# Three 256-column products in place of one of 512 and one of 256, in all feature-major tiles of a two-layer decoder trunk

## The chip, the cores and the metric

The kernel runs on one core of a Trainium2 chip. The metric is the device time of one execution, in microseconds (us), taken as the median of three runs; lower is better. The engines of a core are named as the profile names them: PE (TensorE, the matrix engine), with PEld for its weight loads; DVE (VectorE); ACT (ScalarE); POOL (GpSimd); SP, which here only issues transfers. SBUF is the on-chip memory with 128 partitions, and PSUM is the small memory that PE adds its products into.

## What is computed

The reference is a trunk of two residual layers on 256 tokens of width 2048, all in float32. Each layer is a token mixer (a gMLP in the first, forgetting attention over 16 heads in the second) and then a feed-forward network with a causal convolution of width 3. Cut to the parts that the change touches:

```python
h = h + chunked_gmlp(rmsnorm(h, a_norm), w_in, v_norm, w_s, b_s, w_out)   # u * mixed(v), then w_out
...
def conv_ffn(xn, w_up, conv_w, conv_b, w_down):
    h = xn @ w_up                                   # 2048 -> 2 x 5632
    hp = jnp.pad(h, ((0, 0), (CONV_W - 1, 0), (0, 0)))
    h = sum(hp[:, k:k + S] * conv_w[k] for k in range(CONV_W)) + conv_b
    gate, val = jnp.split(h, 2, axis=-1)
    return (jax.nn.silu(gate) * val) @ w_down       # 5632 -> 2048
...
o = o * jax.nn.sigmoid(g)                           # attention: output gate, then b_w_out
return rmsnorm(h, final_norm)
```

Nearly all the arithmetic is in the matrix products of the 256 tokens with weights that are each used once.

## The kernel before

**Two parts of each number.** The products run in the type float32r, which PE streams in one pass but holds to fewer bits than float32. So every operand is split into a high part (the value rounded to float32r) and a low part (the rest), and a product of two numbers is made of three products of parts: high by high, high by low, low by high. An activation tile such as `X1` is kept as `[P, KD, 2 * T]`: for each block `kt` of 128 features, the first T = 256 columns are the high part for the 256 tokens, the next 256 are the low part. The weights are split while the kernel runs.

**The stream of chunks.** `Stream` (L40) brings in the weights as chunks of 128 x 1024 values (512 KB). In step i it issues the load of chunk i + 6 on the SP queue, splits chunk i + 3 (ACT makes `whi`, L82; DVE makes `wlo`, L83) and emits the products of chunk i, which are PE's. After each chunk's products, `advance` (L57) lets every pending generator take one step: these hold the work that follows a finished tile, and they are how that work is spread over the chunks behind it. The order of each engine's instructions is that in which this code emits them.

**Feature-major tiles.** `feat_block` (L168) computes 256 output features for all 256 tokens: two tiles (m = 0, 1) of 128 features, in the two banks of one PSUM buffer `ps` of shape `[P, 2, 512]`, of which there are three. The weights are the stationary operand, a slice of 128 x 128 from `whi` or `wlo`; the activations are the moving one. A chunk covers four blocks `kt`, so 4 x 2 slices of `whi` and as many of `wlo`. With a slice of `whi`, one product of 512 columns does both parts of the activation at once: columns 0 to 255 of the bank collect what the high activations give, columns 256 to 511 what the low ones give. With a slice of `wlo` a product of 256 columns adds to the first half. I call the first kind wide and the second narrow. The two halves of a bank are added later. In the last chunk of a block the narrow products stand ahead of the wide ones.

Seven weight arrays go through `feat_block`, in this order: `a_in_u` and `a_out` (32 chunks each), `up0` (176), `down0` (88), `b_g` and `b_out` (32 each), `up1` (176), `down1` (88): 656 chunks. One block of them is made otherwise: the last of `down1` (11 chunks) goes through `last_block` (L194), in which every product is narrow, all three kinds add into the first half of the bank, and tile m = 0 of a chunk is done before m = 1, so that the end of the kernel can begin on one tile early (`final_tile`, L317).

**Token-major tiles.** `tok_block` (L215) does `a_in_v`, `b_q`, `kvf_k` and `kvf_v`, 32 chunks each: there the activations are stationary and the weights move, 512 columns at a time. One small chunk, `kvf_f`, goes through `forget` (L547). The change leaves these alone.

**What follows a tile.** Three helpers read `ps` and add its halves:

- `scaled_sum` (L296) for `a_in_u`, `up` and `b_g` (104 blocks): ACT copies the second half of both banks to SBUF (L299, tile `half`), DVE adds the first half (L300), DVE multiplies by `rB`, the token's factor of the RMS norm (L301).
- `residual` (L303) for `a_out`, `down0` and `b_out` (24 blocks): DVE adds the two halves to the residual stream `h` in two steps (L307, L308), and then makes the next `X1`.
- `final` (L332) for blocks 0 to 6 of `down1`: the same by tile, 14 additions on L339 and 14 on L340, with squares on ACT (L341).

Of the kernel before, what the change touches and what calls it, by code (L numbers as in the profile page):

```python
# [17 lines left out]
P = 128  # L18
D = 2048
T = 256  # L20
# [112 lines left out]
def build(ctx, tc, d, out):  # L133
# [31 lines left out]
    def mm(o, a, b, start, stop):  # L165
        nc.tensor.matmul(o, a, b, start=start, stop=stop, skip_group_check=True)  # L166

    def feat_block(src, x, K, done, last=None):  # L168


        if last:
            return last_block(src, x, K, done, last)
        box = {}
        n = K // 4
        for c in range(n):
            def mult(hi, lo, c=c):
                if c == 0:
                    box["ps"] = main_ps()
                ps, xx = box["ps"], x()
                parts = (hi, lo) if c < n - 1 else (lo, hi)  # L180
                for i, part in enumerate(parts):
                    for j in range(4):
                        kt = 4 * c + j
                        for m in range(2):
                            w = part[:, j * 256 + m * P:j * 256 + (m + 1) * P]
                            if part is hi:
                                mm(ps[:, m, :], w, xx[:, kt, :], kt == 0, kt == K - 1)
                            else:
                                mm(ps[:, m, :T], w, xx[:, kt, :T], False, False)
                if c == n - 1:  # L190
                    s.start(done(ps))
            s.chunk(src[c], mult)

    def last_block(src, x, K, done, last):  # L194
        box = {}
        n = K // 4
        for c in range(n):
            def mult(hi, lo, c=c):
                if c == 0:
                    box["ps"] = main_ps()  # L200
                ps, xx = box["ps"], x()
                for m in range(2):
                    for part, half in ((lo, 0), (hi, 1), (hi, 0)):
                        for j in range(4):
                            kt = 4 * c + j
                            mm(ps[:, m, :T], part[:, j * 256 + m * P:j * 256 + (m + 1) * P],
                               xx[:, kt, half * T:(half + 1) * T], part is lo and kt == 0,
                               half == 0 and part is hi and kt == K - 1)
                    if c == n - 1:
                        last(ps, m)  # L210
                if c == n - 1:
                    s.start(done(ps))
            s.chunk(src[c], mult)
# [79 lines left out]
            for i in range(2):  # L293
                nc.vector.tensor_tensor(acc, acc, sq[:, i, :], op=OP.add)

    def scaled_sum(ps, a):  # L296

        t = small.tile([P, 2, T], F32, name="half", tag="half", bufs=2)
        nc.scalar.activation(t, ps[:, :, T:], AF.Copy)  # L299
        nc.vector.tensor_tensor(a, ps[:, :, :T], t, op=OP.add)  # L300
        nc.vector.tensor_tensor(a, a, rB[:, None, :].to_broadcast([P, 2, T]), op=OP.mult)  # L301

    def residual(p, gain):  # L303

        def done(ps):
            hh = h[:, 2 * p:2 * p + 2, :]
            nc.vector.tensor_tensor(hh, hh, ps[:, :, :T], op=OP.add)  # L307
            nc.vector.tensor_tensor(hh, hh, ps[:, :, T:], op=OP.add)  # L308
            for kt in (2 * p, 2 * p + 1):
                prep(X1, kt, gain)  # L310
            square_into_acc(p)
            yield
            if p == 7:
                yield from token_scale()
        return done
# [16 lines left out]
    def final(p, gain):  # L332

        def done(ps):
            kts = (2 * p, 2 * p + 1)
            if p < 7:
                sq = small.tile([P, 2, T], F32, name="sq", tag="sq", bufs=2)
                for m, kt in enumerate(kts):
                    nc.vector.tensor_tensor(h[:, kt, :], h[:, kt, :], ps[:, m, :T], op=OP.add)  # L339
                    nc.vector.tensor_tensor(h[:, kt, :], h[:, kt, :], ps[:, m, T:], op=OP.add)  # L340
                    nc.scalar.activation(sq[:, m, :], h[:, kt, :], AF.Square)  # L341
                if p == 0:
                    nc.vector.tensor_tensor(acc, sq[:, 0, :], sq[:, 1, :], op=OP.add)
                else:
                    for i in range(2):
                        nc.vector.tensor_tensor(acc, acc, sq[:, i, :], op=OP.add)
            for kt in kts:
                nc.scalar.activation(h[:, kt, :], h[:, kt, :], AF.Copy, scale=column(gain + kt))
            if p == 5:
                nc.scalar.activation(warm, ones, AF.Sqrt)  # L350
            if p == 7:
                for m in range(2):
                    sum_tokens(tail["sums"], tail["sq"][:, m, :], False, m == 1)
                v = small.tile([P, 2], F32, name="ts_v", tag="ts_v", bufs=2)
                nc.vector.tensor_scalar(v, tail["sums"][:, :2], 1.0 / D, EPS, op0=OP.mult, op1=OP.add)
                t = small.tile([P, 2], F32, name="rs_t", tag="rs_t2", bufs=2)
                nc.scalar.activation(t, v, AF.Sqrt)
                nc.vector.reciprocal(rcol, t)
                newton(rcol, v, t)
                mp = token_rows()  # L360
                for a, b in ((0, 2), (2, 6), (6, 11), (11, 16)):
                    nc.vector.tensor_tensor(h[:, a:b, :], h[:, a:b, :],  # L362
                                            mp[:, None, :T].to_broadcast([P, b - a, T]), op=OP.mult)
                    nc.sync.dma_start(out[:, a:b, :], h[:, a:b, :])
            yield
        return done
# [68 lines left out]
    def u_done(p):  # L435
        def done(ps):
            X2, vt, wT, bB, _ = mlp_kept()
            u = ph.temp("u", [P, 2, T])
            scaled_sum(ps, u)
            yield  # L440
            nc.scalar.activation(u, u, AF.Gelu)
            mp = misc_ps()
            for m in range(2):
                g = 2 * p + m
                for n in range(2):
                    nc.tensor.matmul(mp[:, m * T + n * P:m * T + (n + 1) * P], vt[:, n, g * P:(g + 1) * P],  # L446
                                     wT[:, g, :], start=True, stop=True)
            mixed = ph.temp("mixed", [P, 2, T])
            for m in range(2):
                g = 2 * p + m  # L450
                nc.vector.scalar_tensor_tensor(
                    mixed[:, m, :].rearrange("p (n t) -> p n t", n=2),
                    mp[:, m * T:(m + 1) * T].rearrange("p (n t) -> p n t", n=2),
                    column(C_AVNORM + g), bB[:, g, None, :].to_broadcast([P, 2, P]), op0=OP.mult, op1=OP.add)
            nc.vector.tensor_tensor(u, u, mixed, op=OP.mult)
            yield
            two_parts(X2[:, 2 * p:2 * p + 2, :], u)
        return done
# [6 lines left out]
    def up_done(l, i):  # L465
        def done(ps):
            state["layer"] = l
            H = ffn_h()
            a = ph.temp("a", [P, 2, T])
            scaled_sum(ps, a)  # L470
            yield
            c = ph.temp("c", [P, 2, T])
            for m in range(2):
                f = m * KF + i
                w = [column(C_CONVW + (l * 3 + k) * 2 * KF + f) for k in range(3)]
                nc.scalar.activation(c[:, m, :], a[:, m, :], AF.Identity, scale=w[2],  # L476
                                     bias=column(C_CONVB + l * 2 * KF + f))
                for k in (1, 0):
                    n = 2 - k
                    nc.vector.scalar_tensor_tensor(c[:, m, n:], a[:, m, :T - n], w[k], c[:, m, n:],  # L480
                                                   op0=OP.mult, op1=OP.add)
            yield
            nc.scalar.activation(c[:, 0, :], c[:, 0, :], AF.Silu)
            nc.vector.tensor_tensor(c[:, 0, :], c[:, 0, :], c[:, 1, :], op=OP.mult)  # L484
            yield
            two_parts(H[:, i, :], c[:, 0, :])
        return done

    def ffn(l, done):
        for i in range(KF):  # L490
            feat_block(d[f"up{l}"][4 * i:4 * i + 4], lambda: X1, KD, up_done(l, i))
        for p in range(8):
            feat_block(d[f"down{l}"][11 * p:11 * p + 11], ffn_h, KF, done(p), final_tile if l and p == 7 else None)


    def att(key):
# [157 lines left out]
    def g_done(p):  # L654
        def done(ps):
            X2, o = att("X2"), att("q")
            gg = ph.temp("big", [P, 512], bufs=6).rearrange("p (a b) -> p a b", a=2)
            scaled_sum(ps, gg)
            yield
            while state["done"] < NH or state["gates"] < p:  # L660
                yield
# [112 lines left out]
```

## Time and profile before

| | |
|---|---|
| runs of the kernel before | 2244.12, 2244.74, 2244.78 us; median 2244.74 us |
| the profiled execution, its own time | 2244.26 us |
| the profiled execution, its span (first to last instruction) | 2242.6 us |
| mean granted clock of PE | 0.998 |
| ACT, busy share of the span | 1193.5 us, 53% |
| products (PE) and weight loads (PEld) | 12546 each |

So 1.66 us of the profiled execution's time lie outside the span, and the median is 0.48 us above that time. The profile gives each instruction a start and a duration. PE's products overlap: the next one begins before the last one's results are out, and the ends are modelled. So PE's speed is not read from its durations but from the distance between the starts of a run of equal products and the start of what comes behind it, divided by the number in the run.

### The profile page before, as it was taken

To read this page: it belongs to the slowest core of one execution; us is meant where nothing else is said; L and a number is where in the kernel's file an instruction comes from. 1 tells how busy PE (TensorE), PEld (TensorE's weight loads), DVE (VectorE), ACT (ScalarE), POOL (GpSimd) and SP (SyncE) were. 2 spreads that over 40 slices of the span, in tenths; PEclk is the share of its full clock that TensorE was granted. 3 is DMA by queue.
4 is the path that set the end of the run, shared out by engine and by line. 5 is a ranking of instruction groups with operands and counts; after the bars stand their busy time and mean duration, and the time that the engine had idled before them with its cause. 6 is when DMAs were issued, how large, how long until landed. Compare 5 with 4: busy or idle time off the path is not lost.

```text
span 2242.6 us, 32429 instructions
## 1 busy us (share of the span) xinstructions
PE 2228.1 (99%) x12546; PEld 1927.1 (86%) x12546; DVE 1528.5 (68%) x2219; ACT 1193.5 (53%) x1625; POOL 19.2 (1%) x41
## 2 busy tenths in 40 slices
PE   9999999999999999999999999999999999999998
PEld 7888888888888888888788888888888888888887
DVE  6566777777777755557786567677777777765554
ACT  6544455555555544445444666446555555544442
POOL 0000000000000000000000110000000000000000
PEclk9999999999999999999999999999999999999999
DMA  8555555656555555555555555555555555565553
GB/s 299 180 187 173 191 190 191 192 190 189 193 191 188 190 183 191 197 190 177 171 183 188 166 168 179 187 189 193 191 188 188 191 191 191 190 196 188 191 190 127
DMA packets 116443, 422.12 MB, mean 188 GB/s; under 512 B 13232, under 2 KB 13376, under 8 KB 116032
## 3 DMA queue, kind: packets, MB, share of 16 engines
q1 hardware_dynamic: 115344, 417.93, 56.7%
q0 software_dynamic: 768, 2.10, 0.3%
q8 instruction: 98, 1.61, 0.3%
q14 instruction: 57, 0.47, 0.1%
q10 hardware_dynamic: 176, 0.02, 0.0%
HBM read 417.88 MB, written 2.11 MB: 187 GB/s over the span
## 4 chain that ended last, share of the span: by engine, by line
PE 99%; DVE 0%; DMA 0%; ACT 0%; SPq 0%; DVEq 0%; issue 0%
PE ps L166 97%; PE mp L446 0%; PE mp L530 0%; PE mp L616 0%; DMA raw<-a_in_v 0%; PE mp L631 0%; PE mp L639 0%; PE mp L640 0%; PE mp L615 0%; PE mp L638 0%; DVE h L362 0%; PE mp L329 0%; PE mp L277 0%; DVE wlo L83 0%; DVEq L768 0%; ACT whi L82 0%
## 5 line engine op out<-in xcount | busy, mean ns | idle before, releaser
L83 DVE TENSOR_TENSOR wlo<-raw,whi 128x1024 fp32r<-128x1024 f32 (+1 forms) x786 | 953.3, 1221 | 378.8 <-ACT whi L82 377.3
L82 ACT ACTIVATE whi<-raw 128x1024 fp32r<-128x1024 f32 (+1 forms) x786 | 822.1, 1054 | 383.2 <-PE ps L166 353.9
L166 PE MATMUL ps<-X,whi 128*128 128x512 f32 x3328 | 829.6, 396 | 0.0
L166 PEld LDWEIGHTS ps<-X,whi 128*128 128x128 f32 x3328 | 602.7, 188 | 120.4
L166 PEld LDWEIGHTS ps<-X,wlo 128*128 128x128 f32 x3328 | 426.2, 188 | 28.1
L166 PE MATMUL ps<-X,wlo 128*128 128x256 f32 x3328 | 430.7, 277 | 0.0
L166 PE MATMUL ps<-ffn_H,whi 128*128 128x512 f32 (+1 forms) x1496 | 355.4, 381 | 0.0
L166 PEld LDWEIGHTS ps<-ffn_H,whi 128*128 128x128 f32 x1496 | 258.7, 188 | 45.3
L299 ACT ACTIVATE half<-ps 128x512 f32<-128x512 f32 x104 | 62.1, 597 | 256.1 <-PE ps L166 256.1
L166 PEld LDWEIGHTS ps<-ffn_H,wlo 128*128 128x128 f32 x1408 | 184.6, 188 | 13.8 <-DVE h L324 0.3
L166 PE MATMUL ps<-ffn_H,wlo 128*128 128x256 f32 x1408 | 188.5, 277 | 0.2 <-DVE h L324 0.2
L300 DVE TENSOR_TENSOR ffn_a<-ps,half 128x512 f32<-128x512 f32 x88 | 60.9, 692 | 175.1 <-ACT half L299 175.1
L166 PE MATMUL ps<-whi,att_X 128*128 128x512 f32 x512 | 168.1, 400 | 0.0
L480 DVE SCALAR_TENSOR_TENSOR ffn_c<-ffn_a,col,ffn_c 128x255 f32<-128x255 f32 x352 | 162.1, 481 | 6.3
L166 PE MATMUL ps<-whi,X 128*128 128x512 f32 x512 | 162.8, 395 | 0.9 <-ACT whi L82 0.9
L476 ACT ACTIVATE ffn_c<-ffn_a,col 128x256 f32<-128x256 f32 x176 | 96.4, 595 | 47.3 <-DVE ffn_a L301 47.3
L166 PEld LDWEIGHTS ps<-whi,X 128*128 128x128 f32 x512 | 96.2, 188 | 21.9 <-ACT whi L82 1.5
L166 PEld LDWEIGHTS ps<-whi,att_X 128*128 128x128 f32 x512 | 96.3, 188 | 20.4
L166 PE MATMUL ps<-wlo,X 128*128 128x512 f32 x256 | 99.7, 390 | 1.0 <-DVE wlo L83 1.0
L166 PE MATMUL ps<-wlo,att_X 128*128 128x512 f32 x256 | 100.0, 391 | 0.0
L245 ACT ACTIVATE X<-h,col 128x256 fp32r<-128x256 f32 x64 | 29.0, 500 | 101.8 <-DVE h L308 99.5
L250 ACT ACTIVATE ffn_H<-ffn_c 128x256 fp32r<-128x256 f32 x88 | 36.7, 418 | 70.2 <-DVE ffn_c L484 70.2
(147 smaller groups left out, 1215.0 us busy)
## 6 DMA issues: line engine op xcount, KB each, us to landing
raw<-up SPq DMA_DIRECT2D x352, 512.0 KB, 3.8
raw<-down SPq DMA_DIRECT2D x176, 512.0 KB, 4.2
raw<-a_in_u SPq DMA_DIRECT2D x32, 512.0 KB, 3.6
raw<-a_out SPq DMA_DIRECT2D x32, 512.0 KB, 4.3
raw<-b_q SPq DMA_DIRECT2D x32, 512.0 KB, 4.2
raw<-kvf_k SPq DMA_DIRECT2D x32, 512.0 KB, 4.0
raw<-kvf_v SPq DMA_DIRECT2D x32, 512.0 KB, 3.6
raw<-b_g SPq DMA_DIRECT2D x32, 512.0 KB, 3.3
```

The costliest lines, as they stand in the source:

```text
L82: self.nc.scalar.activation(hi[:, :n], raw, AF.Copy)
L83: self.nc.vector.tensor_tensor(lo[:, :n], raw, hi[:, :n].bitcast(F32), op=OP.subtract)
L166: nc.tensor.matmul(o, a, b, start=start, stop=stop, skip_group_check=True)
L245: nc.scalar.activation(dst[:, kt, :T], h[:, kt, :], AF.Copy, scale=g)
L250: nc.scalar.activation(dst[..., :T], src, AF.Copy)
L299: nc.scalar.activation(t, ps[:, :, T:], AF.Copy)
L300: nc.vector.tensor_tensor(a, ps[:, :, :T], t, op=OP.add)
L476: nc.scalar.activation(c[:, m, :], a[:, m, :], AF.Identity, scale=w[2], bias=column(C_CONVB + l * 2 * KF + f))
L480: nc.vector.scalar_tensor_tensor(c[:, m, n:], a[:, m, :T - n], w[k], c[:, m, n:], op0=OP.mult, op1=OP.add)
```

## The change

`feat_block` makes no wide products any more. Each slice of `whi` is used for two narrow products one behind the other, one with the high and one with the low half of the activation tile; both add into the first half of the bank, as does the product with `wlo`. Within a chunk all sixteen products with `whi` come first, then the eight with `wlo`, in every chunk. `last_block` is gone: the last block of `down1` goes through the same code, and only in its last chunk is m = 0 completed ahead of m = 1. The second halves of the banks stay unused, so the additions of the halves go: `scaled_sum` becomes `scaled` (one multiplication by DVE out of PSUM), `residual` adds once, and `final` adds and squares both tiles at once.

```diff
-    def feat_block(src, x, K, done, last=None):
-        if last:
-            return last_block(src, x, K, done, last)
+    def feat_block(src, x, K, done, tile_done=None):
...
-                parts = (hi, lo) if c < n - 1 else (lo, hi)
-                for i, part in enumerate(parts):
+
+                def product(part, half, j, m):
+                    kt = 4 * c + j
+                    mm(ps[:, m, :T], part[:, j * 256 + m * P:j * 256 + (m + 1) * P],
+                       xx[:, kt, half * T:(half + 1) * T], kt == 0 and part is hi and half == 0,
+                       kt == K - 1 and part is lo)
+
+                for ms in ((0,), (1,)) if tile_done and c == n - 1 else ((0, 1),):
                     for j in range(4):
-                        kt = 4 * c + j
-                        for m in range(2):
-                            w = part[:, j * 256 + m * P:j * 256 + (m + 1) * P]
-                            if part is hi:
-                                mm(ps[:, m, :], w, xx[:, kt, :], kt == 0, kt == K - 1)
-                            else:
-                                mm(ps[:, m, :T], w, xx[:, kt, :T], False, False)
...
+                        for m in ms:
+                            product(hi, 0, j, m)
+                            product(hi, 1, j, m)
+                    for j in range(4):
+                        for m in ms:
+                            product(lo, 0, j, m)
+                    if tile_done and c == n - 1:
+                        tile_done(ps, ms[0])
...
-    def scaled_sum(ps, a):
-        t = small.tile([P, 2, T], F32, name="half", tag="half", bufs=2)
-        nc.scalar.activation(t, ps[:, :, T:], AF.Copy)
-        nc.vector.tensor_tensor(a, ps[:, :, :T], t, op=OP.add)
-        nc.vector.tensor_tensor(a, a, rB[:, None, :].to_broadcast([P, 2, T]), op=OP.mult)
+    def scaled(ps, a):
+        nc.vector.tensor_tensor(a, ps[:, :, :T], rB[:, None, :].to_broadcast([P, 2, T]), op=OP.mult)
...
             nc.vector.tensor_tensor(hh, hh, ps[:, :, :T], op=OP.add)
-            nc.vector.tensor_tensor(hh, hh, ps[:, :, T:], op=OP.add)
...
-                sq = small.tile([P, 2, T], F32, name="sq", tag="sq", bufs=2)
-                for m, kt in enumerate(kts):
-                    nc.vector.tensor_tensor(h[:, kt, :], h[:, kt, :], ps[:, m, :T], op=OP.add)
-                    nc.vector.tensor_tensor(h[:, kt, :], h[:, kt, :], ps[:, m, T:], op=OP.add)
-                    nc.scalar.activation(sq[:, m, :], h[:, kt, :], AF.Square)
...
+                hh = h[:, 2 * p:2 * p + 2, :]
+                nc.vector.tensor_tensor(hh, hh, ps[:, :, :T], op=OP.add)
+                square_into_acc(p)
```

On PE, this is the second block of `a_in_u` (four chunks, `X_73` being the tile `X1`), up to the small products L446 that mix the tokens of the block before it. Before:

```order
L166 MATMUL ps<-X_73,whi 128x512 x8
L166 MATMUL ps<-X_73,wlo 128x256 x8
L166 MATMUL ps<-X_73,whi 128x512 x8
L166 MATMUL ps<-X_73,wlo 128x256 x16
L166 MATMUL ps<-X_73,whi 128x512 x16
L166 MATMUL ps<-X_73,wlo 128x256 x8
L446 MATMUL mp<-mlp_wT,mlp_vt 128x128 x4
```

The same place now, where the small products have become L419:

```order
L166 MATMUL ps<-X_73,whi 128x256 x16
L166 MATMUL ps<-X_73,wlo 128x256 x8
L166 MATMUL ps<-X_73,whi 128x256 x16
L166 MATMUL ps<-X_73,wlo 128x256 x8
L166 MATMUL ps<-X_73,whi 128x256 x16
L166 MATMUL ps<-X_73,wlo 128x256 x8
```

Each run of 8 wide products has become one of 16 narrow products, and where the last chunk of a block met the one before and after it (the runs of 16 above) the parts now alternate as everywhere else. PE has 5160 products more than before.

On DVE, this is one block of `up0`, from the low part of one chunk to that of the next but three; `ffn_a` is the scaled tile, `ffn_c` the convolution. Before:

```order
L83 TENSOR_TENSOR wlo<-raw,whi 128x1024
L300 TENSOR_TENSOR ffn_a<-ps,half 128x512
L301 TENSOR_TENSOR ffn_a<-ffn_a,rB 128x512
L83 TENSOR_TENSOR wlo<-raw,whi 128x1024
L480 SCALAR_TENSOR_TENSOR ffn_c<-ffn_a,col,ffn_c 128x255
L480 SCALAR_TENSOR_TENSOR ffn_c<-ffn_a,col,ffn_c 128x254
```

And now:

```order
L235 TENSOR_TENSOR ffn_H<-ffn_c,ffn_H 128x256
L83 TENSOR_TENSOR wlo<-raw,whi 128x1024
L282 TENSOR_TENSOR ffn_a<-ps,rB 128x512
L83 TENSOR_TENSOR wlo<-raw,whi 128x1024
L453 SCALAR_TENSOR_TENSOR ffn_c<-ffn_a,col,ffn_c 128x255
L453 SCALAR_TENSOR_TENSOR ffn_c<-ffn_a,col,ffn_c 128x254
```

One of the two DVE operations between the splits is gone, and what is left reads PSUM and `rB` at once; the rest stands as it stood, and so do the transfers.

More of the change, by code (lines that the diff above doesn't have):

```diff
@@ L179, in mult @@
                 ps, xx = box["ps"], x()
-                parts = (hi, lo) if c < n - 1 else (lo, hi)
-                for i, part in enumerate(parts):
-                    for j in range(4):
-                        kt = 4 * c + j
-                        for m in range(2):
-                            w = part[:, j * 256 + m * P:j * 256 + (m + 1) * P]
-                            if part is hi:
-                                mm(ps[:, m, :], w, xx[:, kt, :], kt == 0, kt == K - 1)
-                            else:
-                                mm(ps[:, m, :T], w, xx[:, kt, :T], False, False)
[L190 to L210, printed above, removed]
+                def product(part, half, j, m):
[4 more added lines that the diff above has]
+                for ms in ((0,), (1,)) if tile_done and c == n - 1 else ((0, 1),):
+                    for j in range(4):
+                        for m in ms:
[6 more added lines that the diff above has]
+                        tile_done(ps, ms[0])
                 if c == n - 1:
@@ L336, in done @@
             if p < 7:
-                sq = small.tile([P, 2, T], F32, name="sq", tag="sq", bufs=2)
-                for m, kt in enumerate(kts):
-                    nc.vector.tensor_tensor(h[:, kt, :], h[:, kt, :], ps[:, m, :T], op=OP.add)
-                    nc.vector.tensor_tensor(h[:, kt, :], h[:, kt, :], ps[:, m, T:], op=OP.add)
-                    nc.scalar.activation(sq[:, m, :], h[:, kt, :], AF.Square)
[L342 to L346, printed above, removed]
+                hh = h[:, 2 * p:2 * p + 2, :]
+                nc.vector.tensor_tensor(hh, hh, ps[:, :, :T], op=OP.add)
+                square_into_acc(p)
             for kt in kts:
@@ L438, in done @@
             u = ph.temp("u", [P, 2, T])
-            scaled_sum(ps, u)
+            scaled(ps, u)
             yield
@@ L469, in done @@
             a = ph.temp("a", [P, 2, T])
-            scaled_sum(ps, a)
+            scaled(ps, a)
             yield
@@ L492, in ffn @@
         for p in range(8):
-            feat_block(d[f"down{l}"][11 * p:11 * p + 11], ffn_h, KF, done(p), final_tile if l and p == 7 else None)
+            feat_block(d[f"down{l}"][11 * p:11 * p + 11], ffn_h, KF, done(p),
+                       final_tile if l and p == 7 else None)
     def att(key):
@@ L657, in done @@
             gg = ph.temp("big", [P, 512], bufs=6).rearrange("p (a b) -> p a b", a=2)
-            scaled_sum(ps, gg)
+            scaled(ps, gg)
             yield
```

## The prediction

> **What bounds the kernel now.** I read the first page first, then the table of waits of PE.
>
> ```profile
> PE 2228.1 (99%) x12546; PEld 1927.1 (86%) x12546; DVE 1528.5 (68%) x2219; ACT 1193.5 (53%) x1625; POOL 19.2 (1%) x41
> ...
> PE 99%; DVE 0%; DMA 0%; ACT 0%; SPq 0%; DVEq 0%; issue 0%
> ```
>
> ```profile
> PE mp L382 <- POOL ident L680: 1.5, 1, 1.5
> PE mp L277 <- DVE rcol L263: 1.3, 1, 1.3
> PE ps L166 <- DVE wlo L83: 1.0, 2, 0.8
> PE ps L166 <- ACT whi L82: 0.9, 2, 0.6
> PE mp L329 <- ACT sq L325: 0.6, 1, 0.6
> PE ps L166 <- DVE h L324: 0.2, 1, 0.2
> ```
>
> PE is busy for 99% of the span, the chain of work that ended last runs through PE for 99%, and all of PE's waits come to 5.5 us, at the start and in the tail. So the time is the sum of the distances at which PE can start its products. Work taken from DVE and ACT is worth nothing by itself; what counts is whether two narrow products take longer or shorter than one wide one.
>
> A busy PE hides that price, because the durations overlap. The durations by form:
>
> ```profile
> L166 PE MATMUL ps<-ffn_H,whi 128*128 128x512 f32 x1320 | 331.9, 395 | 0.0
> ...
> L166 PE MATMUL ps<-ffn_H,wlo 128*128 128x256 f32 x1408 | 188.5, 277 | 0.2 <-DVE h L324 0.2
> ```
>
> Read naively, two narrow products (554 ns) cost 159 ns more than a wide one (395 ns). But most of each duration lies beside the next product, so I go to the timeline of PE and read starts. First `down0`, where wide and narrow runs alternate:
>
> ```profile
> 999.74 1.07 PE L166 MATMUL ps<-ffn_H,wlo 128*128 128x256 f32 x8
> 1000.66 2.02 PE L166 MATMUL ps<-ffn_H,whi 128*128 128x512 f32 x8
> 1002.52 1.07 PE L166 MATMUL ps<-ffn_H,wlo 128*128 128x256 f32 x8
> 1003.43 2.02 PE L166 MATMUL ps<-ffn_H,whi 128*128 128x512 f32 x8
> ...
> 1008.06 1.07 PE L166 MATMUL ps<-ffn_H,wlo 128*128 128x256 f32 x8
> ```
>
> Eight wide products take 1002.52 - 1000.66 = 1.86 us, 232.5 ns each; eight narrow ones 0.91 to 0.92 us, some 114 ns each. Twice 114 is 228: the pair is already a little cheaper than the wide product. A chunk takes (1008.06 - 999.74) / 3 = 2.773 us.
>
> Now the last block of `down1`, in which this kernel already does three narrow products per slice:
>
> ```profile
> 2204.81 0.62 PE L166 MATMUL ps<-ffn_H,wlo 128*128 128x256 f32 x4
> 2205.26 1.07 PE L166 MATMUL ps<-ffn_H,whi 128*128 128x256 f32 x8
> 2206.17 0.62 PE L166 MATMUL ps<-ffn_H,wlo 128*128 128x256 f32 x4
> ...
> 2226.57 0.62 PE L166 MATMUL ps<-ffn_H,wlo 128*128 128x256 f32 x4
> ```
>
> From the first row to the last stand 16 groups of 4 + 8 products: 192 in 21.76 us, **113.33 ns each**, without a gap. A chunk of 24 is then 24 x 113.33 = 2.720 us. This is nearly the experiment itself: each product has its own weight load, runs of 12 add into the same columns of one bank, and both halves of the activation tile are read.
>
> **The change part by part.** *The products.* Converted are the 656 feature-major chunks less the 11 of the last block, 645. For the price of a chunk before I check the three chunks above against a whole stage, the longest piece of the chain, from the fifth chunk of `up0` on:
>
> ```profile
> 293.61 726.57 PE ps L166 x4184
> ```
>
> 4184 products are 260 chunks of 16 and 24 wide products of the token-major block behind them. Less 24 x 0.233 = 5.6 us, 721.0 us / 260 = 2.773 us, the same. So 2.773 - 2.720 = 0.053 us are saved for each chunk, 645 x 0.053 = **34.3 us**, about 6.6 ns for each of the 5160 wide products that become pairs.
>
> *How certain 113.33 is in mid-kernel.* The last block has lighter company, as the two stretches show:
>
> ```profile
> 293.00:1020.00 727.00, 727.00 (x4188) 633.07 (x4187) 498.06 (x660) 389.58 (x508) 0.00 (x0) 1.00 0.58 189
> ...
> 2200.00:2227.00 27.00, 27.00 (x240) 27.00 (x240) 11.65 (x13) 9.92 (x12) 0.00 (x0) 1.00 0.27 92
> ```
>
> The columns are length, busy time of PE, PEld, DVE, ACT and POOL, granted clock, DMA share and GB/s. DVE is busy for 69% of the first and 43% of the second, and the transfers are half as dense. A long narrow run in the loaded stage is found where two chunks meet in `up0`:
>
> ```profile
> 600.38 1.98 PE L166 MATMUL ps<-X,wlo 128*128 128x256 f32 x16
> ...
> 602.20 3.89 PE L166 MATMUL ps<-X,whi 128*128 128x512 f32 x16
> ```
>
> Sixteen take 1.82 us, 113.75 ns each. If every product cost that, a chunk would be 2.730 us and the gain 645 x 0.043 = 27.7 us. But 0.01 us of the 1.82 is rounding of the starts, and this run follows a wide one, which the changed kernel no longer has; I take 113.33 and keep 113.75 for the range. From the other side, no row shows narrow products closer than 113 ns.
>
> *New neighbours.* A pair uses the same slice of weights twice, and before every second product the bank changes. No row shows that order. The nearest rows bound it: the last block stays in one bank for 12 products, the `wlo` runs change the bank at each product, and the two are 113.33 and 113.75 ns. The lower end would be a repeated load that is left out; PE's loads are one to a product and hidden already, so I take nothing for it.
>
> *The additions.*
>
> ```profile
> L299 ACT ACTIVATE half<-ps 128x512 f32<-128x512 f32 x104 | 62.1, 597 | 256.1 <-PE ps L166 256.1
> ...
> L300 DVE TENSOR_TENSOR ffn_a<-ps,half 128x512 f32<-128x512 f32 x88 | 60.9, 692 | 175.1 <-ACT half L299 175.1
> ...
> L308 DVE TENSOR_TENSOR h<-h,ps 128x512 f32<-128x512 f32 x24 | 16.5, 686 | 0.8
> ```
>
> Gone are 104 copies on ACT (62 us), 104 additions on DVE (104 x 0.692 = 72 us), the 24 of L308 (16.5 us), and in `final` 28 operations of half the width become 7. All of it lies beside PE, which waited 1.9 us in all for the split parts, at the start. I count nothing. Nothing new stands in its place: the multiplication reads PSUM and `rB` in one operation, for which the nearest row is L300 (PSUM and SBUF, same shape, 692 ns). One thing turns: a buffer `ps` is now released only when `rB` is there. In the first block behind a norm, `rB` is written in the same step of the pending work, just ahead; and `ps` has three buffers, so its next use is two blocks, 22 us, later. No cost.
>
> *Order within a chunk, head and tail.* The high parts are now always needed first and the low ones 16 x 0.113 = 1.8 us later, which suits the order of the splits. The token-major stages, the transfers and the tail from L324 on are the same; in the last block 24 products a chunk stay 24.
>
> *The sum.* 2244.26 (the profiled execution's time) - 34.3 = 2210.0 us. The median of the runs is 0.48 us above that execution, so **2210.4 us**, 1.5% faster.
>
> **The rivals.**
>
> *Narrow products at the loaded price.* All at 113.75 ns: 2244.74 - 27.7 = 2217.0 us. For it: the only narrow runs in a loaded stage show it. Against: the rounding and the wide run ahead.
>
> *A start paid twice (no gain).* A product may have a cost of its own beside its columns, and the split pays it once more. The rows' own measure of a start is the run of 16: 1.82 - 16 x 0.11333 = 0.007 us for one run. Charged to each of the 5160 added products it is 5160 x 6.7 ns = 34.6 us, and the time is 2245.0 us, no change; it breaks even at 6.6 ns. Against it stands the last block, where 192 products in a row carry whatever start there is within their 113.33 ns, and a wide product that costs more than twice that (233 against 226.7). The Trainium skill has such a rule ("TensorE: Matmul & The Clock Gate", section "Back-to-back issue gap"): columns divided by 2.4 GHz, and about 2.5 ns for each product. By it a narrow product is 109.2 ns and a wide one 215.8, so a pair would lose 2.5 ns, 5160 of them 12.9 us, and the kernel would take 2257.6 us. The trace doesn't agree: 113.33 and 233 ns, the wide one 17 ns off the rule and the narrow one 4.
>
> *The supply of instructions (slower).*
>
> ```profile
> q8 instruction: 98, 1.61, 0.3%
> ```
>
> 1.61 MB over 2 x 12546 products and loads are 64 bytes each, so this is PE's program, brought in 98 packets of 256 instructions. 10320 more instructions make 40 more packets, and PE uses 48 instructions in 2.72 us in place of 32 in 2.77, so a packet lasts 14.5 us and not 22.2. Its own time is 0.3% of 16 x 2242.6 us over 98, about 1.1 us. If those 40 all stood open, that would be 44 us: 2210.4 + 44 = 2254 us, slower by 0.4%. It breaks even at 34.3 / 40 = 0.86 us each. Against it: the last block ran at the new rate for 21.8 us, over one packet's worth, without a gap.
>
> *The clock (slower).* PE would stream 1.9% more columns a second in 645 chunks. The granted clock was 1.00 in both stretches above, at the old rate and, for 27 us only, at the new. If a longer stay at the new rate were throttled, the gain would be gone at 2210.4 / 2244.7, a clock of 0.983 of the present one; at 0.97 the time is 2279 us.
>
> **How the numbers follow.** Chances: forecast 0.76, loaded price 0.13, start paid twice 0.04 (half of it at a price above its break-even, and so slower), instructions 0.03, clock 0.02, something unseen about the pairs that takes part of the gain 0.02. The time is that of the likeliest, 2210.4 us. The range takes in the loaded price and a little more above it (2219); below, the rounding of the stage and of the starts (0.05 ns on a narrow product is 0.8 us, 0.005 us on a chunk 3.2 us) gives 2206. A measurement of this kernel can tell about 0.2%, 4.5 us, from no change. Faster by more than that: 0.76 + 0.13 + 0.02 = 0.91; within it 0.02; slower 0.02 + 0.03 + 0.02 = 0.07.
>
> **What would show it.** In the profile after, runs of 16 and 8 narrow products should stand 1.81 and 0.91 us apart in every stage, and a stage of `up` should show 2.720 us for a chunk; PE's products should be 17706 with their total of waits still near 5.5 us; DVE busy about 95 us and ACT about 62 us less, with more idle time and no gain from it; packets of q8 about 138. The prediction is wrong if the runs of 16 take 1.86 us (the pair is no cheaper than the wide product), if gaps appear that no wait explains every 256 instructions, or if the granted clock in the long stages leaves 1.00.

## The result and the profile after

The changed kernel takes 2266.86 us (median of four runs, 2266.84 to 2268.32) against 2244.51 us before on the same chips: a ratio of 1.0101, with a 95% interval of 1.0084 to 1.0119. It is **22.35 us slower**, where 34.3 us faster was forecast. The profiled execution has a span of 2265.1 us, 22.5 us more than before.

The first page of the profile after, its row of busy times, and the table of PE's waits:

```profile
PE 2250.7 (99%) x17706; PEld 2180.2 (96%) x17706; DVE 1444.4 (64%) x2070; ACT 1134.7 (50%) x1514; POOL 19.0 (1%) x41
```

```profile
PE mp L355 <- POOL ident L654: 1.5, 1, 1.5
PE mp L261 <- DVE rcol L247: 1.3, 1, 1.3
PE ps L166 <- DVE wlo L83: 1.0, 2, 0.8
PE mp L309 <- ACT sq L305: 0.6, 1, 0.6
...
```

PE is as busy as it was, it waits no longer than it did (5.1 us in all, with 0.7 us in the two rows not shown), and DVE and ACT have less to do. So the 22 us are in the distance between products. The groups by form show where:

```profile
L166 PE MATMUL ps<-X,whi 128*128 128x256 f32 x6656 | 850.8, 281 | 0.0
...
L166 PE MATMUL ps<-ffn_H,whi 128*128 128x256 f32 x2816 | 360.7, 281 | 0.2 <-DVE h L304 0.2
...
L166 PE MATMUL ps<-mlp_X,whi 128*128 128x256 f32 x512 | 63.3, 277 | 0.0
```

The same narrow product lasts 277 ns on average in `a_out` (activation tile `mlp_X`), as it did on average in the kernel before, and 281 ns in `up` and `down` (most of `X`, and `ffn_H`). The timeline of PE gives the distances, here in `a_out` and then in `up0`:

```profile
250.11 1.07 PE L166 MATMUL ps<-mlp_X,wlo 128*128 128x256 f32 x8
251.02 1.98 PE L166 MATMUL ps<-mlp_X,whi 128*128 128x256 f32 x16
252.83 1.07 PE L166 MATMUL ps<-mlp_X,wlo 128*128 128x256 f32 x8
...
602.79 1.11 PE L166 MATMUL ps<-X,wlo 128*128 128x256 f32 x8
603.74 2.05 PE L166 MATMUL ps<-X,whi 128*128 128x256 f32 x16
605.62 1.11 PE L166 MATMUL ps<-X,wlo 128*128 128x256 f32 x8
```

From one narrow `wlo` run to the next, a chunk is 252.83 - 250.11 = 2.72 us in `a_out`: exactly the forecast. In `up0` it is 605.62 - 602.79 = 2.83 us, in runs of both kinds alike. The chain of work gives the distances for whole stages:

```profile
194.05 89.78 PE ps L166 x792
290.14 740.54 PE ps L166 x6264
...
1368.85 141.46 PE ps L166 x1248
1516.62 733.53 PE ps L166 x6228
```

In the first and third row (`a_out` with the start of `up0`; the rest of `b_g`, `b_out` and the start of `up1`) a product takes 89.78 us / 792 = 113.36 ns and 141.46 / 1248 = 113.35 ns. In the second (`up0` and `down0`, with 24 token-major products, 5.6 us, taken off) it is 734.9 / 6240 = **117.78 ns**, and in the fourth 733.53 / 6228 = 117.78 ns. There are two distances, **113.3 and 117.8 ns**, and nothing between: in the whole trace, every uninterrupted run of 24 narrow products or more settles at one of the two within 0.1 ns. At the longer one a chunk is 24 x 117.78 = 2.827 us, 0.054 us more than the 2.773 us with wide products: as much as the shorter one saves.

Where does it change? These are the second, third and the start of the fourth chunk of `up0`, in the timeline of PE:

```profile
280.94 1.98 PE L166 MATMUL ps<-X,whi 128*128 128x256 f32 x16
282.75 1.07 PE L166 MATMUL ps<-X,wlo 128*128 128x256 f32 x8
283.66 0.50 PE L309 MATMUL mp<-ones,acc 128*128 128x1 f32 x4
284.02 2.13 PE L166 MATMUL ps<-X,whi 128*128 128x256 f32 x16
285.99 1.11 PE L166 MATMUL ps<-X,wlo 128*128 128x256 f32 x8
286.93 2.05 PE L166 MATMUL ps<-X,whi 128*128 128x256 f32 x16
```

The chunk ahead of L309 has 16 products of `whi` in 282.75 - 280.94 = 1.81 us; in the chunk behind it eight of `wlo` already take 286.93 - 285.99 = 0.94 us, 117.5 ns each. L309 is `token_sums`: two one-column float32 products, each of which stands in the trace as two records, that the RMS norm of the residual stream puts between two chunks. Two chunks later come the two transposes of `token_rows` (L261), and from there on 6240 products, 735 us without an interruption, keep 117.8 ns. Tile, code and weight array are the same on both sides of L309.

### The profile page after: what moved, and what is told of

It is laid out like the page before. It is cut to its first block, busy times and chain, and to the rows that moved or that the text cites. A ratio compares the mean times of both kernels' runs of the same rounds, so it can differ in the third digit from the quotient of the medians.

```text
span 2265.1 us, 42572 instructions
## 1 busy us (share of the span) xinstructions
PE 2250.7 (99%) x17706; PEld 2180.2 (96%) x17706; DVE 1444.4 (64%) x2070; ACT 1134.7 (50%) x1514; POOL 19.0 (1%) x41
## 4 chain that ended last, share of the span: by engine, by line
PE 99%; DVE 0%; DMA 0%; ACT 0%; SPq 0%; DVEq 0%; issue 0%
PE ps L166 97%; PE mp L419 0%; PE mp L504 0%; PE mp L590 0%; DMA raw<-a_in_v 0%; PE mp L605 0%; PE mp L614 0%; PE mp L613 0%; PE mp L589 0%; PE mp L612 0%; DVE h L335 0%; PE mp L309 0%; PE mp L261 0%; DVE wlo L83 0%; DVEq L742 0%; ACT whi L82 0%
## 5 line engine op out<-in xcount | busy, mean ns | idle before, releaser
L166 PE MATMUL ps<-X,whi 128*128 128x256 f32 x6656 | 850.8, 281 | 0.0
L166 PEld LDWEIGHTS ps<-X,whi 128*128 128x128 f32 x6656 | 809.8, 189 | 0.4
L166 PE MATMUL ps<-X,wlo 128*128 128x256 f32 x3328 | 458.2, 281 | 0.0
L166 PEld LDWEIGHTS ps<-X,wlo 128*128 128x128 f32 x3328 | 419.7, 189 | 0.0
L166 PE MATMUL ps<-ffn_H,whi 128*128 128x256 f32 x2816 | 360.7, 281 | 0.2 <-DVE h L304 0.2
L166 PEld LDWEIGHTS ps<-ffn_H,whi 128*128 128x128 f32 x2816 | 344.1, 189 | 0.3 <-DVE h L304 0.3
L166 PE MATMUL ps<-ffn_H,wlo 128*128 128x256 f32 x1408 | 194.9, 281 | 0.0
L282 DVE TENSOR_TENSOR ffn_a<-ps,rB 128x512 f32<-128x512 f32 x88 | 60.8, 691 | 129.0 <-PE ps L166 125.0
L166 PE MATMUL ps<-att_X,whi 128*128 128x256 f32 (+1 forms) x528 | 68.9, 280 | 0.0
L166 PEld LDWEIGHTS ps<-att_X,whi 128*128 128x128 f32 (+1 forms) x528 | 61.9, 185 | 2.0
```

The source lines that it names most:

```text
L282: nc.vector.tensor_tensor(a, ps[:, :, :T], rB[:, None, :].to_broadcast([P, 2, T]), op=OP.mult)
```

## The experiments

**The theory** they test I call the sticky spacing: a run of narrow products falls into one of two spacings when it starts, and stays in it until something else runs on PE; behind a wide product it falls into the short one. In the kernel before, all but 4 of the 515 narrow runs of eight products or more stood right behind a wide one. The rivals: the longer spacing belongs to the stage (its tiles, or what the other engines do there), or it is the price of the new pairs, which use one slice of weights twice in a row.

The part on wide products is too simple, as the trace of the kernel before shows, again behind `token_sums` (there L329):

```profile
287.17 0.50 PE L329 MATMUL mp<-ones,acc 128*128 128x1 f32 x4
287.53 2.10 PE L166 MATMUL ps<-X,whi 128*128 128x512 f32 x8
289.48 2.05 PE L166 MATMUL ps<-X,wlo 128*128 128x256 f32 x16
291.36 2.03 PE L166 MATMUL ps<-X,whi 128*128 128x512 f32 x8
```

Eight wide products stand ahead of the 16 narrow ones, and these still take (291.36 - 289.48) / 16 = 117.5 ns. Of the 511 runs behind wide products in that trace six are at the longer spacing, and of the other four runs three; together they are 88 products, or 0.4 us. So the longer spacing was there before the change, but no such run was longer than 16 products.

**e1_wide: six extra wide products.** Their results are read by nobody.

```diff
+    def reset(n):
+        mm(misc_ps()[:, :n], X1[:, 0, :P], X1[:, 0, :n], True, True)
     def token_scale():
         yield
         token_sums()
+        reset(512)
         yield
         yield
         nc.scalar.activation(rB, token_rows()[:, :T], AF.Copy)
+        reset(512)
```

> The changed kernel, with one more product of 512 columns (X1 by itself, into a buffer that nobody reads) behind each token_sums and each token_rows of token_scale: six in all, some 0.35 us each. Sticky spacing (two spacings, 113.3 and 117.8 ns, one of them taken when a run of narrow products starts and kept until something else runs on PE; behind a wide product it is 113.3): up0, down0, up1 and down1 go from 117.8 to 113.3 ns, 12564 products x 4.43 ns = 55.7 us less, 2 us for the six, so about 2213 us, faster than before. Rival, the spacing belongs to the stage (its tiles, or the load of the other engines there): 2269 us, the spacing stays 117.8. Rival, the pair that uses one slice twice is what costs: 2269 us as well.

Measured: **2212.23 us** (four runs, 2211.94 to 2212.64), ratio to the kernel before 0.9858, interval 0.9841 to 0.9874. That is 54.6 us less than the changed kernel and 32 us less than the kernel before. The same place in its timeline, and the pieces of its chain for the two layers:

```profile
283.60 0.50 PE L314 MATMUL mp<-ones,acc 128*128 128x1 f32 x4
283.96 0.48 PE L166 MATMUL mp<-X 128*128 128x512 f32 x1
284.27 1.98 PE L166 MATMUL ps<-X,whi 128*128 128x256 f32 x16
286.09 1.07 PE L166 MATMUL ps<-X,wlo 128*128 128x256 f32 x8
```

```profile
290.33 712.70 PE ps L166 x6264
...
1489.69 705.86 PE ps L166 x6228
```

Behind the one product of 512 columns, 16 narrow ones take 286.09 - 284.27 = 1.82 us, and the long pieces are 27.84 and 27.67 us shorter: 707.1 / 6240 = 113.3 ns in all of `up0` and `down0`. Both rivals expected 2269 us and are out: stage, tiles and pairs are what they were.

**e2_narrow: the control,** the same six with `reset(256)` in place of `reset(512)`.

> The control for the kernel with six wide products: the same six, but of 256 columns. Sticky spacing with only a wide product as the reset: the product is one more of the narrow run, the spacing stays 117.8 ns in up and down, 2268 us. If any product at that place would do, or if the spacing is drawn anew by chance at each interruption: up or down at 113.3 ns, 2213 us if all are. Rivals (stage, pair): 2268 us.

Measured: 2212.0 us (one run). My expectation of 2268 us was wrong, and the trace says why (the runs behind the two extra products of the first layer):

```profile
284.16 2.04 PE L166 MATMUL ps<-X,whi 128*128 128x256 f32 x16
286.04 1.10 PE L166 MATMUL ps<-X,wlo 128*128 128x256 f32 x8
...
290.15 1.99 PE L166 MATMUL ps<-X,whi 128*128 128x256 f32 x16
291.98 1.07 PE L166 MATMUL ps<-X,wlo 128*128 128x256 f32 x8
```

Behind `token_sums` the narrow product leads to the longer spacing (1.88 us for 16), behind `token_rows` to the shorter (1.83 us, with the first ones still settling), and the latter holds for the long stretch. Both layers agree. So a narrow product can also end in the short spacing; it depends on what stands ahead of it. Behind `token_sums`, e1_wide and e2_narrow differ in the width of one product alone (113.3 ns behind 512 columns, 117.8 behind 256), so the place in the program isn't what decides there. Is a wide product any surer?

**e3_switch: extra products ahead of single blocks,** in the changed kernel.

```diff
+                    if ahead:
+                        aside(*ahead)
                     box["ps"] = main_ps()
...
+    def aside(kind, n):
+        mp = misc_ps()
+        for i in range(n):
+            if kind == "one":
+                nc.tensor.matmul(mp[:, i:i + 1], ident, ones[:, :1], start=True, stop=True)
+            else:
+                mm(mp[:, :kind], X1[:, 0, :P], X1[:, 0, :kind], True, True)
```

> The changed kernel with extra products ahead of some blocks of up0 and up1, whose results nobody reads. up0, by block: 4 one of 512 columns, 8 four of one column, 12 one of 384, 16 four of one column, 20 one of 256, 24 one of 512, 28 a single one of one column, 32 one of 512, 36 four of 128, 40 one of 512. up1: 4 one of 512, 8 four of one column, 12 one of 512, 16 four of one column, 20 one of 512, 24 four of one column, 28 one of 448, 32 four of one column, 36 one of 320, 40 two of 512. Sticky spacing: 113.3 ns from each 512 on, 117.8 from the four of one column on, at once and until the next extra product, each time; 256 leaves 117.8; for 384, 448, 320, four of 128 and the single one it has no forecast, and the run shows where the line lies. Rivals (stage, pair): 117.8 ns throughout up0 and up1.

Measured: 2224.76 us (one run). Half of what I expected came. The first 512 of each layer switches to 113.3 ns at once; but none of the six groups of four one-column products in `up0` and `up1` switches back, nor does the single one, nor 384, 448, 320 or four of 128 columns. One does that I had down as harmless: the narrow product of 256 columns, at block 20 of `up0`, behind which the chain has the longer piece for the same 384 products (500.92), until the next 512 ends it:

```profile
290.53 33.92 PE ps L170 x288
324.69 43.53 PE ps L170 x384
...
500.92 45.23 PE ps L170 x384
546.37 43.53 PE ps L170 x384
```

43.53 / 384 = 113.4 ns, 45.23 / 384 = 117.8 ns. So small products of one kind do not always lead to the long spacing; the ones of `token_sums` do where they stand.

**e4_oldtail: the kernel before, disturbed.** Four one-column products (eight records) ahead of its last block, from which the forecast took its price.

```diff
                 if c == 0:
+                    mp = misc_ps()
+                    for i in range(4):
+                        nc.tensor.matmul(mp[:, i:i + 1], ident, ones[:, :1], start=True, stop=True)
                     box["ps"] = main_ps()
```

> The kernel before, with four products of one column ahead of its last block, the one with narrow products alone from which the forecast took 113.33 ns. Sticky spacing: that block goes from 113.3 to 117.8 ns, 264 x 4.43 ns = 1.2 us longer, some 2246 us with the four; the order of its products, without pairs, makes no difference. Rival, the pair: 113.3 ns as before, 2245 us. Rival, the stage: 113.3 ns, since nothing else there changes.

Measured: 2246.74 us (one run) against 2244.38 us before. The last block in its timeline:

```profile
2199.76 0.95 PE L202 MATMUL mp<-ones,ident 128*128 128x1 f32 x8
...
2202.06 0.63 PE L166 MATMUL ps<-ffn_H,wlo 128*128 128x256 f32 x4
2202.53 1.11 PE L166 MATMUL ps<-ffn_H,whi 128*128 128x256 f32 x8
...
2206.30 0.63 PE L166 MATMUL ps<-ffn_H,wlo 128*128 128x256 f32 x4
```

From 2202.06 to 2206.30 stand three groups of 4 + 8, 36 products in 4.24 us: 117.8 ns, where the untouched kernel has 113.33. There are no pairs in this block. My forecast rested on a number that four small products ahead of it change by 4%.

**e5_sizes: which widths set which spacing.** As e3_switch, with another list of extra products.

> Again the changed kernel with one extra product ahead of some blocks, all of the kind X1 by itself; the two up stages begin at 117.8 ns. up0, by block: 4 one of 288 columns, 8 of 256, 12 of 320, 16 of 256, 20 of 384, 24 of 256, 28 of 448, 32 of 256, 36 of 512, 40 of 256. up1: 4 of 256, 8 of 512, 12 of 256, 16 of 512, 20 of 256, 24 of 512, 28 of 256, 32 of 512, 36 of 256, 40 of 512. If a wide product always leads to 113.3 ns and does so because it lets the weight load get ahead (a load takes 188 ns, and ends 40 ns before its product begins behind a wide one, but 73 to 78 ns after that behind a narrow one): 512 and 448 always give 113.3, and the smaller ones less surely as they come near 256. If the narrow one of 256 is a setter of 117.8: 117.8 behind each of them. If 256 only disturbs, and either spacing can come out: some of its sites at 113.3 and some at 117.8, while each 512 still gives 113.3. Rival, any extra product draws the spacing anew: 512 too would leave 117.8 at some of its six sites.

Measured: 2249.35 us (one run). The blocks behind each extra product, 384 narrow ones to a row; in this order behind 256, 384, 256, 448, 256 and 512 columns (the three rows ahead of them, behind 288, 256 and 320, are at the longer spacing too):

```profile
...
460.82 45.23 PE ps L170 x384
506.22 43.52 PE ps L170 x384
549.86 45.23 PE ps L170 x384
595.29 45.23 PE ps L170 x384
640.64 45.23 PE ps L170 x384
686.09 43.53 PE ps L170 x384
```

From the long spacing, 288, 320 and 448 columns lead nowhere, 384 and 512 to the short one. In both layers together, 512 did so at six sites of six here, and the extra 256 led to (or left) the long spacing at all ten, six of these from the short one. So it isn't drawn by chance, and it isn't simply a matter of how wide the extra product is: that 384 resets and 448 doesn't, each at the one site where it was tried from the long spacing, speaks against my idea that a product resets by giving the weight load time to get ahead.

**e6_tok and e7_wide_again: can more be had, and does it hold?** e6_tok has the wide product behind `token_rows` alone, and splits the token-major products as well, two of twelve left wide in each chunk:

```diff
-                        mm(ps[:, tb, :], a, hi[:, w], kt == 0, False)
-                        mm(ps[:, tb, :], a, lo[:, w], False, False)
-                        mm(ps[:, tb, :], b, hi[:, w], False, kt == KD - 1)
+                        if j == 0:
+                            mm(ps[:, tb, :], a, hi[:, w], kt == 0, False)
+                            rest = ((a, lo), (b, hi))
+                        else:
+                            rest = ((a, hi), (a, lo), (b, hi))
+                        for x_, w_ in rest:
+                            for q in range(2):
+                                mm(ps[:, tb, q * T:(q + 1) * T], x_, w_[:, j * 512 + q * T:j * 512 + (q + 1) * T],
+                                   False, kt == KD - 1 and x_ is b)
```

> The changed kernel with one wide product behind each token_rows of token_scale (none behind token_sums), and the token-major products split too: of the twelve products of 512 columns of a chunk, two stay wide (the first high by high of each half of the tokens) and ten become two of 256 each. Sticky spacing: a chunk of 12 wide ones at about 230 ns (2.755 us) becomes 2 x 232 + 20 x 113.3 + some 10 ns of getting into step behind each wide one, 2.75 us: between nothing and 0.04 us saved in each of 128 chunks, 2207 to 2213 us. If the narrow spacing behind the small products of those stages is 117.8 at times, the wide ones in each chunk should set it back within a chunk. If narrow products with moving weights are slower than 115 ns: above 2213 us.

> The same kernel as e1_wide, for a comparison with e6_tok on one chip, and to see whether the spacing comes out the same in every execution: 2212 us in each, if a wide product sets it; some executions near 2240 us (one layer at 117.8 ns) if it is drawn by chance.

Measured on one chip, four runs each: e6_tok 2217.63 us (2217.41 to 2224.03; ratio 0.9892, interval 0.9875 to 0.9908), e7_wide_again 2213.16 us (2212.07 to 2215.07; ratio 0.9863, interval 0.9849 to 0.9878). Splitting the token-major products loses 4.5 us where nothing to 5 us were to be gained. The first such stretch, in its chain, took 44.62 us for what took 43.99 us in e1_wide. The timeline of the second shows why (a row of `whi` with x4 and the two products of `wlo` behind it are six narrow products):

```profile
63.03 0.63 PE L166 MATMUL ps<-whi,X 128*128 128x256 f32 x4
...
63.74 0.63 PE L166 MATMUL ps<-whi,X 128*128 128x256 f32 x4
...
65.85 0.62 PE L166 MATMUL ps<-whi,X 128*128 128x256 f32 x4
...
66.53 0.62 PE L166 MATMUL ps<-whi,X 128*128 128x256 f32 x4
```

Six products take 63.74 - 63.03 = 0.71 us, 118 ns each; shortly after, with two wide products between, six take 66.53 - 65.85 = 0.68 us, 113 ns each. In the four token-major arrays together, 82 of the 127 runs of 16 narrow products that the trace shows are at the longer spacing, though a wide product stands right ahead of each. With the runs of 4, most of which are at it too, these are some 1790 products, 8 us at 4.45 ns each, against the up to 5 us to be gained. So the wide products did not set the spacing back, against my expectation, and a wide product doesn't always lead to the short one. The kernel with six wide products repeats its time, and in none of its runs a layer falls back by 27 us.

**e8_one: a single extra wide product,** behind the first `token_rows`.

```diff
         nc.scalar.activation(rB, token_rows()[:, :T], AF.Copy)
+        if "reset" not in tail:
+            tail["reset"] = True
+            mm(misc_ps(), X1[:, 0, :P], X1[:, 0, :], True, True)
```

> The changed kernel with a single extra wide product, behind the first token_rows of token_scale, ahead of the third block but one chunk of up0. Sticky spacing: the 6240 narrow products of up0 and down0 behind it go from 117.8 to 113.3 ns and those of up1 and down1 stay at 117.8: 2266.9 - 6240 x 4.43 ns + 0.35 us = 2239.6 us, one product of 0.2 us worth 27 us. If the spacing came from the load of the other engines or from the tiles: 2267 us.

Measured: 2241.63 us (one run). The chain has the one layer at one spacing and the other at the other:

```profile
11.31 46.38 PE ps L166 x191
...
292.94 712.70 PE ps L166 x6264
...
1491.57 733.54 PE ps L166 x6228
```

740.54 - 712.70 = 27.84 us for one product. The 2 us over the expected 2239.6 are in the first row: the same 191 token-major products took 44.00 us in the changed kernel. The granted clock was 0.92 from 12 to 30 us in this execution and 1.00 there in that of the changed kernel, and the extra product stands 280 us later; so the excess has nothing to do with the edit.

**e9_adds: the removed work put back,** in e1_wide, on data that nobody uses.

```diff
+        t = small.tile([P, 2, T], F32, name="half", tag="half", bufs=2)
+        nc.scalar.activation(t, ps[:, :, :T], AF.Copy)
+        nc.vector.tensor_tensor(t, ps[:, :, :T], t, op=OP.add)
         nc.vector.tensor_tensor(a, ps[:, :, :T], rB[:, None, :].to_broadcast([P, 2, T]), op=OP.mult)
...
+            t = small.tile([P, 2, T], F32, name="half", tag="half", bufs=2)
+            nc.vector.tensor_tensor(t, hh, ps[:, :, :T], op=OP.add)
             nc.vector.tensor_tensor(hh, hh, ps[:, :, :T], op=OP.add)
```

> The kernel with six wide products (e1_wide, 2212 us) with the work on ACT and DVE that the change took away put back, on data that nobody uses: in scaled a copy of ps by ACT and an addition by DVE, as before the change in shape and order, and in residual a second addition by DVE. The forecast counted this work as nothing: 2212 us, with DVE and ACT busy as much as before the change, and 113.3 ns in all stages. If the work is worth something to PE, or if its load on memory changes the spacing: above 2216 us.

Measured: 2212.23 us (2211.98 to 2214.70), ratio 0.9860, interval 0.9844 to 0.9876: the same median as without it. Its row of busy times has nearly the load of the kernel before again (the additions of `final` stay out):

```profile
PE 2196.4 (99%) x17712; PEld 2125.1 (96%) x17712; DVE 1512.9 (68%) x2198; ACT 1193.3 (54%) x1618; POOL 19.9 (1%) x41
```

So the additions that `scaled` and `residual` lost are worth nothing, and the load of DVE and ACT doesn't set the spacing.

## Why the prediction was wrong

**The step that failed** is the one on how certain 113.33 ns is in mid-kernel. I took the price of a narrow product from the last block of the kernel before and treated it as a property of the product, with 113.75 ns, from a run in a loaded stage, as its upper end. It is a property of the run: 113.3 or 117.8 ns, by what ran on PE ahead of it. Both of my rows were in the short spacing, and the upper end rested on one of them alone; the run of 16 at 289.48 in the same trace, shown above, has 117.5 ns. I even wrote that the run at 600.38 "follows a wide one, which the changed kernel no longer has", and read it as a reason for the cheaper price, which nothing here bears out. What the change takes away is the wide products that ended each narrow run after 16 products at most, outside the last block. A start in the longer spacing cost 16 products in the kernel before; now it lasts for a whole layer. Whether the wide products or the two transposes behind them ended it there, the runs do not separate. The sum then comes out by itself: 34.3 us forecast, less 4.45 ns (117.78 - 113.33) for each of the 12564 products behind `token_sums` and `token_rows` in both layers (48 + 6240 + 48 + 6228), 55.9 us, is 21.6 us slower. In the trace after, 8 of the 32 chunks of `b_g`, between the heads of the attention, are at the longer spacing as well, 192 products or 0.85 us; the 0.4 us of the kernel before go off. That is 22.1 us; the spans differ by 22.5 us.

**What held.** At 113.3 ns the gain is there: `a_out` has its 2.72 us a chunk, and with six products to set the spacing the kernel takes 2212.23 us, 1.8 us from the 2210.4 us forecast, about what the six cost (six at 0.31 us, 284.27 - 283.96). It is close in part by luck, since those 8 chunks of `b_g` stay at the longer spacing there too. The pairs cost nothing of their own (113.3 ns with pairs in `a_out`, 117.8 ns without pairs in e4_oldtail). The additions put back in e9_adds cost nothing. Order within the chunk, waits and tail were as said.

**The rivals.** The loaded price isn't what happened: e9_adds has the full load and 113.3 ns, and in the run at 600.38 itself only the first step is longer (118 ns), the others are at 113.3 ns on average. The start paid twice would have given about no change by its row, and it has the wrong form: nothing is added to a product as such. The rule of the Trainium skill quoted there ("TensorE: Matmul & The Clock Gate", section "Back-to-back issue gap"), which that section gives for an isolated product, came to 2257.6 us, nearer to the result than my forecast, but by 109.2 and 215.8 ns, neither of which any stage here shows; the two spacings are not in it. The supply of instructions is out: the page after counts 138 packets on that queue, as forecast, and PE has no new gaps. The clock is out: it stands at 1.00 in the long stages of both kernels. (Its break-even was worked out wrongly: 2210.4 / 2244.7 is 0.985, not 0.983.) None of the rivals named a cost that depends on what came before, and that is where the missing chance should have gone.

**What stays open.** Why there are two spacings, and what decides between them at a start. The runs show that the outcome is the same each time at a given place, that it is settled within the first few products behind the start, that an extra product of 512 columns led to the short one at every site in `up` where it was tried, though wide products elsewhere do not (e6_tok; six runs of the kernel before), that an extra 256 in mid-run led to the long one at every site, and that neither the width alone (384 against 448) nor the kind of the small products (four of one column: short spacing at six sites in `up`, long one in e4_oldtail) tells it. The profile's records don't show the inside of PE.

## What to carry to other kernels

Where PE is the bound, measure its price by the distance between starts in a long run, and look for more than one such distance for one and the same form; the mean duration in the groups gives it away (277 against 281 ns here). Before a price from one stage is carried to another, compare what stands ahead of the run in both, not only what stands in it. A kernel of long uniform runs can hang by a few ns at their start for hundreds of us, so after such a change look at the instructions that interrupt the runs: one extra product of 512 columns behind them was worth 27.8 us here. And read all such runs of the profile at hand, not one: the longer spacing stood in it.

## What the runs showed that I had not expected

- Two spacings for one form of product, 113.3 and 117.8 ns, each kept for up to 6240 products (735 us at the longer) and the same in repeated executions.
- A wide product is dearer than two narrow ones at the short spacing (233 against 226.7 ns) and cheaper than two at the long one (235.6 ns). So 512 against 256 columns cannot be ranked without the spacing.
- One extra product of 256 columns, in the middle of a run of its own kind, moved the whole run from the short to the long spacing at seven sites of seven; one of 384 columns moved it back, one of 448 didn't.
- The best versions found are the change plus six products that compute nothing: 2212.23 us with 512 columns, 1.4% under the kernel before, and 2212.0 us in the one run with 256.
